# Half of the up projection's low weight parts made by an adding transfer in place of VectorE's subtraction

## The chip, the core and the metric

The kernel runs on one core of one Trainium2 chip. The metric is device time in microseconds (us): three runs of the kernel before took 1555.34, 1555.97 and 1557.21 us, median 1555.97. Beside them stands one profiled execution, from which all rows of the profile come.

## The reference, cut to what matters

The reference is one decoder layer on 256 tokens of 2048 channels in float32: two token mixers (a gated linear recurrence and a sliding-window attention), a gated merge, an output projection, and a squared-ReLU MLP with 8192 hidden channels. The change is in the MLP's first product:

```python
h = rmsnorm(x, norm_mlp_pre[l])
u = jnp.square(jax.nn.relu(h @ w_mlp_up[l]))          # 2048 -> 8192, the up projection
x = x + rmsnorm(u @ w_mlp_down[l], norm_mlp_post[l])  # 8192 -> 2048
```

## The kernel before, in words

Every weight goes through TensorE as two float32r numbers. The high part is the weight rounded to float32r, the low part is what the rounding left (weight minus high part), and a product is put together from matmuls on the high part and on the low part. So each weight is read from memory once and then split on the core.

**The weight stream.** The class `Stream` (line 52) holds all weights as one list of chunks of 128 x 2048 float32 in the order in which TensorE uses them. Each chunk is handled as two halves of 128 x 1024 (512 KB), numbered j = 0, 1, 2 and so on. Three steps stand behind a half:

- `load_to` (L74): SyncE's queue (SP) loads the half into a tile `wraw`. There are WRAW = 4 such buffers for the stream.
- `two_parts` (L92): ScalarE (ACT) copies `wraw` into `whi`, which rounds it to float32r. There are WHALF = 6 buffers of `whi`.
- `two_parts` (L93): VectorE (DVE) subtracts `whi` from `wraw` into `wlo`, of which there are 6 buffers too. With that the `wraw` buffer is free for a later load.

`ahead` runs this up to AHEAD = 6 halves before the half that TensorE (PE) works on; the free buffers decide the rest. A `whi` buffer comes free when PE has done the high matmuls of the half six places earlier, a `wlo` buffer when it has done the low ones.

**The up projection.** It is done in two rounds, f = 0 and f = 1, each of 32 chunks, 64 halves, and each followed by two passes of the down projection over the hidden channels of that round. `a_pair` (line 225) takes four halves: for each half eight matmuls of 512 columns on `whi` (L235), then eight of 256 columns on `wlo` (L238), into the accumulator `ps`. After four halves ScalarE and VectorE take `ps` out (L242, L243), and `evacuate` (L936 to L951) applies ReLU, scale and square and splits the result for the down projection. At the start of f = 0 ScalarE and VectorE also finish the first residual (L914 to L918), which ScalarE's queue stores in eight transfers; the accumulators and that residual are loaded back (L1056, L1057) when the last down passes begin.

**Order.** Each engine works its instructions off in the order in which they stand. A scheduler in the framework sets that order when the program is built, from its own estimates, and it also decides which free buffer a load gets; the kernel pins only a few places. Waits between engines are semaphores. GpSimd (POOL) does four of the low parts at the very start of the program and nothing in the up projection.

Of the kernel before, what the change touches and what calls it, by code (L numbers as in the profile page):

```python
# [16 lines left out]
F32 = mybir.dt.float32  # L17
# [3 lines left out]
ALU = mybir.AluOpType  # L21
# [30 lines left out]
class Stream:  # L52
# [3 lines left out]
    def __init__(self, nc, pool, chunks, room, sums):  # L56
        self.nc, self.pool, self.chunks, self.room, self.sums = nc, pool, chunks, room, sums
        self.raw, self.parts = {}, {}
        self.loaded = self.split = 0
        self.pin = lambda i: i  # L60
        self.low = nc.vector
        self.at = 0

    def load_to(self, n):
        while self.loaded < min(n, 2 * len(self.chunks)):
            j = self.loaded
            c = slice(j % 2 * 1024, j % 2 * 1024 + 1024)
            if j < 2 * EXTRA:
                if j % 2 == 0:
                    self.place = self.room(f"wraw{j}")  # L70
                t = self.place[:, c]
            else:
                t = self.pool.tile([P, 1024], F32, tag="wraw", bufs=WRAW, name=f"wraw{j}")
            self.nc.sync.dma_start(t, self.chunks[j // 2][:, c])  # L74
            self.raw[j] = t
            self.loaded += 1
# [12 lines left out]
    def two_parts(self, src, j):  # L89
        hi = self.pool.tile([P, 1024], F32R, tag="whi", bufs=WHALF, name=f"whi{j}")  # L90
        lo = self.pool.tile([P, 1024], F32R, tag="wlo", bufs=WHALF, name=f"wlo{j}")
        self.pin(self.nc.scalar.copy(hi, src))  # L92
        self.pin(self.low.tensor_tensor(lo, src, hi.bitcast(F32), ALU.subtract))  # L93
        return hi, lo

# [55 lines left out]
def layer(tc, x, pos_t, pos_row, inv_freq, vecs, sinks, gains, w_kv, w_q, w_xy, w_rg, w_g, w_rp, w_ap, w_out,  # L151
# [14 lines left out]
    chunks = [w_kv[i] for i in range(4)]  # L166
# [17 lines left out]
            chunks += [w_g[2 * p + 4], w_g[2 * p + 5]]  # L184
    chunks += [w_out[i] for i in range(16)]
    sums = set()
    for f in range(2):
        chunks += [w_up[32 * f + i] for i in range(32)]
        for n in range(2):
            sums.update(len(chunks) + i for i in SEVEN)  # L190
            chunks += [w_dn[(2 * f + n) * PAIRS + i] for i in range(PAIRS)]

    def unit(name, dt=F32R):
        return big.tile([P, 4, 2, S], dt, tag="U8", name=name)

    def flat(t):
        return t.rearrange("p a b c -> p (a b c)")

    ws = Stream(nc, wpool, chunks, lambda name: flat(unit(name, F32)), sums)

    def units(name):
        return [unit(f"{name}{i}") for i in range(4)]
# [585 lines left out]
    for p in range(8):  # L788
# [8 lines left out]
        hi = mixT[p // 2][:, e : e + 2, 0, :]  # L797
# [222 lines left out]
    for f in range(2):  # L1020
# [3 lines left out]
        for p in range(PAIRS):  # L1024
# [8 lines left out]
            if f == 1 or p >= R2_AT:  # L1033
                for q, u in full:
                    if q in SEVEN:
                        uT[q] = pc.tile([P, 2, 7, P], F32R, tag="seven", bufs=len(SEVEN), name=f"seven{f}{q}")
                    else:
                        i = sum(k not in SEVEN for k in range(q))
# [136 lines left out]
```

## Time and profile before

| | us |
|---|---|
| runs, median of 3 | 1555.97 |
| profiled execution: span from first to last instruction | 1551.8 |
| PE busy | 1520.3 (98%) |
| DVE busy | 1119.6 (72%) |
| ACT busy | 842.6 (54%) |
| POOL busy | 12.1 (1%) |
| L92 `whi`, 528 instructions, mean 1.050 | 548.9 |
| L93 `wlo` on DVE, 524 instructions, mean 1.223 | 635.6 |
| first load of the up weights issued at / last | 815.7 / 1344.5 |

The profiled execution gives its span only; the median of the runs is 4.2 us above it, which is what lies around the span. A row of a group reads: line, engine, operation, output and input tiles, shape, count, busy time and mean ns, then the engine's idle time just before these instructions and what ended it. A row of windows gives the busy time of each engine in a stretch of the span, with the granted clock of TensorE and the busy share of the 16 transfer engines. The two stretches in which PE works on the up projection run from about 847 to 1003 us (f = 0, its first halves split earlier) and from about 1190 to 1370 us (f = 1).

### The profile page before, as it was taken

To read this page: it belongs to the slowest core of one execution; us is meant where nothing else is said; L and a number is where in the kernel's file an instruction comes from. 1 tells how busy PE (TensorE), PEld (TensorE's weight loads), DVE (VectorE), ACT (ScalarE), POOL (GpSimd) and SP (SyncE) were. 2 spreads that over 40 slices of the span, in tenths; PEclk is the share of its full clock that TensorE was granted. 3 is DMA by queue.
4 is the path that set the end of the run, shared out by engine and by line. 5 is a ranking of instruction groups with operands and counts; after the bars stand their busy time and mean duration, and the time that the engine had idled before them with its cause. 6 is when DMAs were issued, how large, how long until landed. Compare 5 with 4: busy or idle time off the path is not lost.

```text
span 1551.8 us, 20965 instructions
## 1 busy us (share of the span) xinstructions
PE 1520.3 (98%) x8042; PEld 1288.1 (83%) x8042; DVE 1119.6 (72%) x1370; ACT 842.6 (54%) x1148; POOL 12.1 (1%) x14
## 2 busy tenths in 40 slices
PE   7999999999999999999999999999999999999996
PEld 5887777788888888888787888888888888888884
DVE  6666667866858877555656876688886766779987
ACT  4545655646647766444354655555454555555552
POOL 3000000000000000000000000000000000000000
PEclk8999999999999999999999999999999999999999
DMA  6554354354655466555663865556667655576564
GB/s 246 170 170 147 125 168 158 126 188 150 227 188 173 162 216 195 190 186 190 252 226 103 274 202 188 189 181 209 212 208 237 205 191 187 182 282 195 202 210 128
DMA packets 82326, 296.26 MB, mean 191 GB/s; under 512 B 9521, under 2 KB 9777, under 8 KB 81201
## 3 DMA queue, kind: packets, MB, share of 16 engines
q1 hardware_dynamic: 78768, 285.48, 56.0%
q10 hardware_dynamic: 3458, 9.45, 1.7%
q8 instruction: 63, 1.03, 0.3%
q14 instruction: 37, 0.30, 0.1%
HBM read 288.60 MB, written 6.29 MB: 190 GB/s over the span
## 4 chain that ended last, share of the span: by engine, by line
PE 83%; DVE 7%; ACT 4%; DMA 4%; issue 2%; POOL 0%; DVEq 0%; ACTq 0%; POOLq 0%
PE ps L235 35%; PE ps L238 18%; PE dQ L956 5%; PE s L956 3%; DVE wlo L93 3%; DMA wraw<-in_w_dn 3%; PE dP L956 3%; PE dCs L956 2%; PE o L253 2%; PE o L255 2%; PE o L257 2%; PE q L253 2%; PE q L255 2%; PE q L257 2%; ACT whi L92 2%
## 5 line engine op out<-in xcount | busy, mean ns | idle before, releaser
L93 DVE TENSOR_TENSOR wlo<-wraw,whi 128x1024 fp32r<-128x1024 f32 x524 | 635.6, 1223 | 312.1 <-ACT whi L92 309.5
L92 ACT CAST whi<-wraw 128x1024 fp32r<-128x1024 f32 x528 | 548.9, 1050 | 571.2 <-PE ps L235 259.7
L235 PE MATMUL ps<-hT,whi 128*128 128x512 f32 x1024 | 261.2, 395 | 0.0
L235 PE MATMUL ps<-h2T,whi 128*128 128x512 f32 x1024 | 256.6, 392 | 0.6 <-DVE h2T L282 0.6
L235 PEld LDWEIGHTS ps<-hT,whi 128*128 128x128 f32 x1024 | 183.8, 189 | 36.0 <-issue 3.1
L235 PEld LDWEIGHTS ps<-h2T,whi 128*128 128x128 f32 x1024 | 184.2, 189 | 33.8 <-DVE h2T L282 0.8
L238 PEld LDWEIGHTS ps<-hT,wlo 128*128 128x128 f32 x1024 | 139.9, 190 | 10.6 <-issue 0.8
L238 PEld LDWEIGHTS ps<-h2T,wlo 128*128 128x128 f32 x1024 | 139.7, 190 | 10.0
L238 PE MATMUL ps<-hT,wlo 128*128 128x256 f32 x1024 | 144.1, 283 | 0.0
L238 PE MATMUL ps<-h2T,wlo 128*128 128x256 f32 x1024 | 142.8, 282 | 0.0
L956 PE MATMUL dQ<-whi,uT 128*128 128x512 f32 x288 | 107.0, 390 | 0.8 <-ACT whi L92 0.8
L235 PE MATMUL ps<-yrnn,whi 128*128 128x512 f32 x256 | 64.4, 393 | 0.7 <-DVE yrnn L748 0.7
L956 PEld LDWEIGHTS dQ<-whi,uT 128*128 128x128 f32 x288 | 54.2, 188 | 12.4 <-ACT whi L92 1.3
L235 PE MATMUL ps<-yatt,whi 128*128 128x512 f32 x256 | 64.1, 392 | 0.0
L956 PE MATMUL dQ<-wlo,uT 128*128 128x512 f32 x144 | 56.5, 392 | 4.0 <-DVE wlo L93 4.0
L112 DVE TENSOR_TENSOR tlo<-t,thi 128x1536 fp32r<-128x1536 f32 x28 | 49.2, 1757 | 9.5 <-ACT thi L111 9.5
L956 PE MATMUL dCs<-whi,uT 128*128 128x512 f32 x144 | 54.6, 396 | 0.0
L956 PE MATMUL dP<-whi,uT 128*128 128x512 f32 x144 | 53.8, 389 | 0.0
L235 PEld LDWEIGHTS ps<-yrnn,whi 128*128 128x128 f32 x256 | 46.0, 189 | 9.3 <-DVE yrnn L748 1.1
L235 PEld LDWEIGHTS ps<-yatt,whi 128*128 128x128 f32 x256 | 46.0, 189 | 8.3
L253 PE MATMUL q<-whi,hT 128*128 128x512 f32 x128 | 51.1, 399 | 0.0
L255 PE MATMUL q<-wlo,hT 128*128 128x512 f32 x128 | 50.4, 393 | 0.0
(255 smaller groups left out, 2068.8 us busy)
## 6 DMA issues: line engine op xcount, KB each, us to landing
wraw<-in_w_up SPq DMA_DIRECT2D x128, 512.0 KB, 4.6
wraw<-in_w_dn SPq DMA_DIRECT2D x128, 512.0 KB, 4.5
wraw<-in_w_g SPq DMA_DIRECT2D x64, 512.0 KB, 4.7
wraw<-in_w_xy SPq DMA_DIRECT2D x64, 512.0 KB, 4.5
wraw<-in_w_q SPq DMA_DIRECT2D x32, 512.0 KB, 4.4
wraw<-in_w_ap SPq DMA_DIRECT2D x32, 512.0 KB, 4.7
wraw<-in_w_rp SPq DMA_DIRECT2D x32, 512.0 KB, 4.8
wraw<-in_w_out SPq DMA_DIRECT2D x32, 512.0 KB, 5.2
```

What stands on the lines that cost most here:

```text
L92: self.pin(self.nc.scalar.copy(hi, src))
L93: self.pin(self.low.tensor_tensor(lo, src, hi.bitcast(F32), ALU.subtract))
L112: v.tensor_tensor(lo, t, hi.bitcast(F32), ALU.subtract)
L235: mm(both, hi[:, k * P : k * P + P], a.rearrange("p a b -> p (a b)"), start=half == 0 and k == 0, stop=False)
L238: mm(ps[:, f, 1, :], lo[:, k * P : k * P + P], a[:, 0, :], start=False, stop=half == 1 and k == 7)
L253: mm(banks[tb][n], a[:, 0, t], hi[:, n * 512 : n * 512 + 512], start=first, stop=False)
L255: mm(banks[tb][n], a[:, 0, t], lo[:, n * 512 : n * 512 + 512], start=False, stop=False)
L257: mm(banks[tb][n], a[:, 1, t], hi[:, n * 512 : n * 512 + 512], start=False, stop=last)
L956: mm(b, a[x], w[y], start=not begun and i == 0, stop=tail and i == 2)
```

## The change

For every odd half of the up projection, 64 of its 128, VectorE's subtraction is taken out. ScalarE writes minus the high part into `wlo` right after it has made `whi`, and a transfer issued by GpSimd adds the raw weights onto it in SBUF (`accum_op=ALU.add`). The sum is the same low part. The even halves, and all other weights, are split as before. In the new file ScalarE's copy stands in L93, its multiplication by -1 in L95, GpSimd's transfer in L96 and VectorE's subtraction in L98.

```diff
     def __init__(self, nc, pool, chunks, room, sums):
...
         self.at = 0
+        self.by_dma = set()
...
         self.pin(self.nc.scalar.copy(hi, src))
+        if j in self.by_dma:
+            self.nc.scalar.mul(lo, hi.bitcast(F32), -1.0)
+            self.nc.gpsimd.dma_start(lo.bitcast(F32), src, accum_op=ALU.add)
+            return hi, lo
         self.pin(self.low.tensor_tensor(lo, src, hi.bitcast(F32), ALU.subtract))
         return hi, lo
...
     sums = set()
+    by_dma = set()
     for f in range(2):
+        by_dma.update(2 * (len(chunks) + i) + 1 for i in range(32))
         chunks += [w_up[32 * f + i] for i in range(32)]
...
     ws = Stream(nc, wpool, chunks, lambda name: flat(unit(name, F32)), sums)
+    ws.by_dma = by_dma
```

The scheduler sets the orders anew. Three places of the up projection show what moved. The numbers behind the tile names are the half (`whi297` is half 297) and then a running number; the names in brackets are the semaphores that an instruction waits for (DMAHW and DMASW: transfers of SP or ACT, and of GpSimd).

ScalarE's queue before, in the middle of f = 0:

```order
L92 CAST whi296_7970<-wraw296_7878 128x1024 [waits DMAHW6_49,PE_49]
L92 CAST whi297_8007<-wraw297_7908 128x1024 [waits DMAHW7_49,PE_49]
L242 COPY u_7902<-ps_7903 128x512 [waits PE_49]
L92 CAST whi298_8029<-wraw298_7930 128x1024 [waits DMAHW0_49,PE_49]
L938 ACTIVATE u_7902<-u_7902 128x512 [waits DVE_49]
L950 CAST seven04_7994<-u_7902 128x384 [waits Activation_49]
L92 CAST whi299_8051<-wraw299_7952 128x1024 [waits DMAHW1_49,PE_49]
L950 CAST seven04_7994<-e_7997 128x512 [waits DVE_49]
L92 CAST whi300_8073<-wraw300_7974 128x1024 [waits DMAHW2_49,PE_49]
```

The same place of ScalarE's queue now:

```order
L93 CAST whi296_7982<-wraw296_7888 128x1024 [waits DMAHW6_49,PE_49]
L93 CAST whi297_8019<-wraw297_7919 128x1024 [waits DMAHW7_49,PE_49]
L250 COPY u_7912<-ps_7913 128x512 [waits PE_49]
L95 ACTIVATE wlo297_8020<-whi297_8019 128x1024 [waits DMASW1_49,Activation_49]
L93 CAST whi298_8042<-wraw298_7941 128x1024 [waits DMAHW0_49,PE_49]
L946 ACTIVATE u_7912<-u_7912 128x512 [waits DVE_49]
L958 CAST seven04_8006<-u_7912 128x384 [waits Activation_49]
L93 CAST whi299_8064<-wraw299_7964 128x1024 [waits DMAHW1_49,PE_49]
L958 CAST seven04_8006<-e_8009 128x512 [waits DVE_49]
L95 ACTIVATE wlo299_8065<-whi299_8064 128x1024 [waits DMASW2_49,PE_49,Activation_49]
L93 CAST whi300_8087<-wraw300_7986 128x1024 [waits DMAHW2_49,PE_49]
```

The multiplication stands between the copy of its own half and that of the next, once behind the copy of `ps` and once behind a cast. GpSimd's queue now holds the adding transfers alone, one for each odd half; before it held nothing here:

```order
L96 DMA wlo293_7915<-wraw293_7821 128x1024 [waits DMASW7_49,DMAHW3_49,PE_49,Activation_49]
L96 DMA wlo295_7960<-wraw295_7866 128x1024 [waits DMAHW5_49,DMASW0_49,Activation_49]
L96 DMA wlo297_8020<-wraw297_7919 128x1024 [waits DMASW1_49,DMAHW7_49,PE_49,Activation_49]
L96 DMA wlo299_8065<-wraw299_7964 128x1024 [waits DMAHW1_49,DMASW2_49,Activation_49]
L96 DMA wlo301_8118<-wraw301_8024 128x1024 [waits DMASW3_49,DMAHW3_49,PE_49,Activation_49]
```

Each transfer waits for the one that filled its `wlo` buffer three odd halves earlier, so `wlo299` waits on DMASW2 for the transfer into `wlo293`, and DMASW2 is the semaphore of half 293, DMASW3 that of half 295. SP's queue, which loads `wraw`, before:

```order
L74 DMA wraw304_8077<-in_w_up 128x1024 [waits DMAHW2_49,DVE_49]
L74 DMA wraw305_8107<-in_w_up 128x1024 [waits DMAHW3_49,DVE_49]
L74 DMA wraw306_8129<-in_w_up 128x1024 [waits DMAHW4_49,DVE_49]
L74 DMA wraw307_8151<-in_w_up 128x1024 [waits DMAHW5_49,DVE_49]
L74 DMA wraw308_8173<-in_w_up 128x1024 [waits DMAHW6_49,DVE_49]
```

SP's queue now:

```order
L75 DMA wraw296_7888<-in_w_up 128x1024 [waits DMAHW1_49,DMASW1_49]
L75 DMA wraw297_7919<-in_w_up 128x1024 [waits DMAHW4_49,DVE_49]
L75 DMA wraw298_7941<-in_w_up 128x1024 [waits DMAHW3_49,DMASW2_49]
L75 DMA wraw299_7964<-in_w_up 128x1024 [waits DMAHW6_49,DVE_49]
L75 DMA wraw300_7986<-in_w_up 128x1024 [waits DMAHW5_49,DMASW3_49]
```

Before, every load waited for VectorE to release the buffer used four halves earlier. Now the load of an even half, 298, takes the buffer of the odd half five places earlier, 293, and waits for that half's adding transfer; the load of an odd half takes the buffer of the even half three places earlier and waits for VectorE.

## The prediction on record

> **What bounds the kernel now.** I read the page first, then the busy times by window over the two stretches of the up projection, then the waits in a quiet part of them, then the timeline of one half, and last the transfers.
>
> ```profile
> span 1551.8 us, 20965 instructions
> PE 1520.3 (98%) x8042; PEld 1288.1 (83%) x8042; DVE 1119.6 (72%) x1370; ACT 842.6 (54%) x1148; POOL 12.1 (1%) x14
> ```
>
> ```profile
> 847.00:1003.00 156.00, 155.39 (x890) 136.67 (x890) 115.23 (x147) 92.82 (x126) 0.00 (x0) 1.00 0.66 211
> 1190.00:1370.00 180.00, 180.00 (x1028) 158.18 (x1028) 125.92 (x149) 99.50 (x121) 0.00 (x0) 1.00 0.60 194
> ```
>
> The columns of a window are its bounds and length, then the busy time of PE, weight load, DVE, ACT and POOL, the granted clock, the share of the 16 transfer engines, and GB/s. TensorE is busy 155.39 of 156 us and 180 of 180 us in the two up stretches, at full clock. Nothing there waits for VectorE or ScalarE but one matmul, at the beginning:
>
> ```profile
> PE ps L235 <- DVE h2T L282: 0.6, 1, 0.6
> ```
>
> Next, in a stretch of 60 us, who waits for whom:
>
> ```profile
> ACT whi L92 <- PE ps L235: 27.5, 22, 1.7
> DVE wlo L93 <- ACT whi L92: 20.1, 22, 1.6
> ```
>
> ScalarE waits for TensorE to release a `whi` buffer, and VectorE waits for ScalarE. The splitting runs as far ahead as its buffers let it, and TensorE sets the pace. The timeline shows one half:
>
> ```profile
> 911.75 1.05 ACT L92 CAST whi<-wraw 128x1024 fp32r<-128x1024 f32 x1 [1.22 <-PE ps L235]
> 912.50 2.00 PE L235 MATMUL ps<-h2T,whi 128*128 128x512 f32 x8
> 912.83 1.22 DVE L93 TENSOR_TENSOR wlo<-wraw,whi 128x1024 fp32r<-128x1024 f32 x1 [0.97 <-ACT whi L92]
> 914.08 3.12 SPq L74 DMA_DIRECT2D wraw<-in_w_up  x2
> 914.34 1.12 PE L238 MATMUL ps<-h2T,wlo 128*128 128x256 f32 x8
> 914.54 1.05 ACT L92 CAST whi<-wraw 128x1024 fp32r<-128x1024 f32 x1 [1.74 <-PE ps L235]
> 915.30 2.00 PE L235 MATMUL ps<-h2T,whi 128*128 128x512 f32 x8
> 915.50 0.59 ACT L242 COPY u<-ps 128x512 f32<-128x512 f32 x1
> ```
>
> A half takes 2.80 us of TensorE (912.50 to 915.30). The subtraction that ends at 914.05 frees a `wraw` buffer and SP issues the next load at 914.08. The high matmuls that end at 914.34 free a `whi` buffer, and the copy begins at 914.54; since there are six buffers, that copy is for the half that TensorE reaches at 912.50 + 6 x 2.80 = 929.30.
>
> **What is removed.** 64 subtractions on VectorE:
>
> ```profile
> L93 DVE TENSOR_TENSOR wlo<-wraw,whi 128x1024 fp32r<-128x1024 f32 x524 | 635.6, 1223 | 312.1 <-ACT whi L92 309.5
> L92 ACT CAST whi<-wraw 128x1024 fp32r<-128x1024 f32 x528 | 548.9, 1050 | 571.2 <-PE ps L235 259.7
> ```
>
> 64 x 1.223 = 78 us of VectorE, which was busy 115 + 126 = 241 of 336 us there and kept nobody waiting. What this can give back is bounded by TensorE's idle time in the stretches: 0.6 us. I take 0.
>
> **What is added on ScalarE.** 64 multiplications of the shape of L92, so 64 x 1.05 = 67 us on an engine busy 92.8 + 99.5 = 192 of 336 us. It would be busy 259, 77%. Each one waits for the low matmuls of the half six earlier, and behind it in the queue stands the next copy. In the timeline the copy ends at 915.59, that `wlo` buffer came free at 915.30, and the copy of `ps` adds 0.59, so the multiplication runs from 916.2 to 917.2. The next copy may begin at 914.54 + 2.80 = 917.34 at the earliest, since it waits for TensorE. The cost is 0, hidden under that wait; without this cover it would be 1.05 us per odd half, 67 us, on an engine that still has 77 us to spare. Placed as it is, I expect none of it on the path.
>
> **What is added on GpSimd and the transfer engines.** 64 transfers of 512 KB that read `wraw`, read `wlo` and write `wlo`. GpSimd stands idle (0.00 in both windows), so nothing is queued behind its waiting instruction but the next such transfer. Two things depend on when the transfer lands: TensorE's low matmuls of that half, and SP's load that takes the `wraw` buffer.
>
> For the matmuls there is room. The multiplication ends at 917.2 and the low matmuls come at 929.30 + 1.84 = 931.1, so the transfer may take 13.9 us.
>
> For the buffer it is tighter. By the order, an even half's buffer goes to the odd half three later, and an odd half's to the even half five later. Two tenancies follow each other in each buffer in 8 halves, or 22.4 us of TensorE. In them stand two loads, two copies, one subtraction, one multiplication and one adding transfer. The loads' durations, from the quiet stretch (920 to 980 us) and from the crowded one (850 to 890 us), in KB and median us to landing:
>
> ```profile
> wraw<-in_w_up SPq DMA_DIRECT2D x22, 512.0 KB, 4.7
> ```
>
> ```profile
> wraw<-in_w_up SPq DMA_DIRECT2D x17, 512.0 KB, 6.3
> ```
>
> ```profile
> 850.00:890.00 40.00, 40.00 (x234) 35.30 (x233) 34.20 (x48) 27.85 (x47) 0.00 (x0) 1.00 0.86 277
> 920.00:980.00 60.00, 60.00 (x347) 52.89 (x346) 39.63 (x50) 32.56 (x40) 0.00 (x0) 1.00 0.57 186
> ```
>
> With the transfer engines 57% busy a load lands in 4.7 us, with 86% in 6.3 us. The adding transfers raise the share from 57%, so I take 5.5, the middle. The sum for 8 halves without the transfer: loads 2 x 5.5 = 11.0, copies 2 x 1.05 = 2.10, subtraction 1.23, multiplication 1.05, half of the 0.59 copy of `ps` = 0.30 (it stands ahead of every second multiplication), and four hand-overs of about 0.1 = 0.4. That is 16.1 us, and leaves 6.3 us for the adding transfer.
>
> No row shows an adding transfer. From below, it is a 512 KB transfer, and the fastest load in the up stretch landed in 3.6 us:
>
> ```profile
> DMA to landing us min/median/max: 3.6/4.7/6.4
> ```
>
> From above, it reads 1024 KB, and the transfers of 1024 KB took:
>
> ```profile
> x<-in_x SPq DMA_DIRECT2D x2, 1024.0 KB, 7.7
> ...
> acc<-acc_away ACTq DMA_DIRECT2D x2, 1024.0 KB, 11.3
> x<-x_away ACTq DMA_DIRECT2D x2, 1024.0 KB, 14.7
> g<-in_gains SPq DMA_DIRECT2D x1, 1024.0 KB, 6.8
> gp<-in_gains SPq DMA_DIRECT2D x1, 1024.0 KB, 10.7
> ```
>
> So it lies between 3.6 and 14.7 us. It cannot be below nothing, since the buffer waits for it in any case. I take 8.5: nearest to the 7.7 and 6.8 of the 1024 KB loads, which also read 1024 KB, and somewhat above, because it runs among other loads all the time, as those of 10.7 and 11.3 did.
>
> That makes 16.1 + 8.5 = 24.6 us for 8 halves against 22.4, 2.2 us too long. Over 128 halves it is 16 x 2.2 = 35 us. Part of it is taken by the lead: the low part may land 13.9 us after the multiplication and needs 8.5, so each stretch can fall behind by 5.4 us before TensorE stands, 10.8 in both. Net: 35 - 10.8 = **24 us**, as waits of TensorE for `whi` and `wlo` late in each stretch. Against the profiled execution: 1551.8 + 24 = 1576 us of span, and with the 4.2 us by which the median of the runs, 1555.97, stands above its span, **1580 us**.
>
> This mechanism's own range: with 5.1 for a load and 7.7 for the transfer the sum is 15.3 + 7.7 = 23.0, 0.6 too long, 10 us in all, which the lead of 2 x 6.2 swallows; with 6.3 and 10.7 it is 17.7 + 10.7 = 28.4, 6.0 too long, 96 - 6 = 90 us. So 1558 to 1646.
>
> **Rival 1: the transfer is hidden.** If it lands within 6.3 us, the two tenancies fit into 22.4 us and TensorE never waits: 1556 us. What speaks for it: TensorE's lead of six halves, the load's own 4.7, and 43% of the transfer engines free. Against it: two reads, and a row at 850 to 890 us where loads alone, with 256 KB stores beside them, already need 86%. There the transfers of the first halves come on top, and the cost may be a few us even then; it is the point at which this case would turn into slower by over 0.2%. The Trainium skill, "DMA: Bandwidth & Descriptors", section "Anatomy of one DMA — SWDGE (gpsimd) path", gives 2.0 us plus bytes over 436 GB/s for a transfer issued by GpSimd, an estimate of 3.2 us here; by that rule the sum is 16.1 + 3.2 = 19.3 and the time 1556. The trace has no such transfer, but its loads, 4.7 us for the same bytes from another queue, are 1.5 us above that estimate, and the rule is for a plain copy. Chance 0.30, of which 0.05 goes to slower by the crowded start.
>
> **Rival 2: the transfer engines become the bound.** What counts then is not how long a transfer takes but how much of the 16 engines.
>
> ```profile
> q1 hardware_dynamic: 3058, 11.12, 57.1%
> ```
>
> ```profile
> 10.00:15.00 5.00, 4.19 (x14) 1.99 (x12) 2.75 (x4) 1.21 (x2) 0.00 (x0) 0.83 1.03 418
> ```
>
> In 60 us 11.12 MB are 21.2 loads of 0.524 MB, and 57.1% of 60 us is 34.3, so a load holds the engines for 1.62 us. With many loads in flight, at the program's start, they moved 418 GB/s, so a load needs at least 1.25 us. Four halves are 11.2 us. Four loads at 1.25 leave 6.2, 3.1 for each of two adding transfers. One that costs a single pass, 1.25, or two, 2.5, fits; three passes of 1.62, 4.9, do not. With 4.0 it would be 5.0 + 8.0 = 13.0, 1.8 too long, 32 x 1.8 = 58, less 10.8 of lead: 47 us, 1603. With 4.9 it is 14.8, 115 - 11 = 104 us, 1660. For it speaks that two reads are needed; against it that source and target lie on the core. The Trainium skill, "Collectives: The Full Stack", section "The bandwidth ceiling: the fold count and why AG ≠ RS ≠ AR", says that an add in a transfer engine costs a second source read and halves the rate; by it an estimate of 2.5 to 3.2 us follows, at the edge of 3.1. No run here shows an add yet. Chance 0.18.
>
> **Rival 3: faster.** VectorE's 78 us free would have to shorten a path on which TensorE waits: the 0.6 us at the start of f = 0, and whatever order the scheduler finds at the edges of the down passes. More than 3 us can hardly come of it. Price -3 us, 1553. Chance 0.05.
>
> **How the numbers follow.** The forecast has 0.47, rival 1 0.30, rival 2 0.18, rival 3 0.05. About 0.2% (3 us) is what a measurement of this kernel can tell from no change. Faster: 0.05. Within it: 0.25. Slower: 0.47 + 0.18 + 0.05 = 0.70. The range reaches from 1553, which takes in the hidden case and rival 3's price, to 1646, the upper end of the forecast's own range; it leaves out the upper part of rival 2 and little else.
>
> **What would show each step.** Right: in the changed profile, L98 in place of L93 with 460 instructions on VectorE, 64 multiplications of 1.05 us, waits of SP's loads of even halves on GpSimd's transfers, ScalarE's copies waiting for `in_w_up` loads where they now wait for PE, and TensorE idle in both up stretches, more towards their ends. In the stretch 920 to 980 the transfer engines should be over 80% busy. Wrong: TensorE at 60 of 60 us there and copies that still wait for PE (rival 1, a landing under 6.3 us); a share of 1.0 with loads landing in 7 us or more (rival 2); ScalarE's multiplications late because TensorE's `wlo` buffers hold them, or GpSimd taking several us to issue one transfer, would be costs that this sum lacks.

## The result: 4.2% slower, and the profile after

The changed kernel takes 1621.0 us (median of 4 runs, 1617.28 to 1629.78) against 1556.6 us: a ratio of 1.0422, interval 1.0403 to 1.0442, or +64 us where +24 was forecast. The time lies in the stated range and on the forecast side of no change, but the loss is 2.7 times the forecast one. The profiled execution has a span of 1618.5 us, 66.7 more than before. Its run took 1620.25 us, so only 1.8 us lie around the span; if it is as much before, the rest of the 4.2 us by which the median there stands above its span is scatter between executions.

Its page, engines first, then the two transfer queues that matter, and the costliest lines:

```profile
span 1618.5 us, 21129 instructions
PE 1543.0 (95%) x8042; PEld 1297.8 (80%) x8042; DVE 1046.5 (65%) x1306; ACT 901.8 (56%) x1212; POOL 67.8 (4%) x78
...
q1 hardware_dynamic: 78768, 285.48, 53.0%
q0 software_dynamic: 9216, 33.56, 11.3%
...
PE 68%; DMA 18%; DVE 5%; issue 5%; ACT 4%; POOL 0%; SPq 0%; DVEq 0%; POOLq 0%; ACTq 0%
...
L98 DVE TENSOR_TENSOR wlo<-wraw,whi 128x1024 fp32r<-128x1024 f32 x460 | 557.9, 1223 | 404.5 <-ACT whi L93 399.7
...
L96 POOL DMA_DIRECT2D wlo<-wraw x64 | 55.6, 869 | 1335.1 <-PE ps L243 854.6
...
L95 ACT ACTIVATE wlo<-whi 128x1024 fp32r<-128x1024 f32 x64 | 67.7, 1058 | 1.0 <-ACT whi L93 0.4
```

The 64 subtractions are gone, the 64 multiplications take 1.06 us each, GpSimd spends 0.87 us on each issue, and transfers now carry 18% of the chain that ends last, against 4%. TensorE is busy 22.7 us longer for the same 8042 matmuls and idle 44.0 us longer. The windows tell where. First the two up stretches of before, then of after, then the first 16 us behind each up stretch of after (columns as in the prediction; a share over 1 can occur because a transfer is counted in the window in which it begins):

```profile
847.70:1027.00 179.30, 179.30 (x1028) 157.81 (x1029) 134.46 (x167) 105.80 (x142) 0.00 (x0) 1.00 0.64 207
1192.10:1370.80 178.70, 178.70 (x1025) 157.27 (x1024) 125.72 (x148) 98.48 (x120) 0.00 (x0) 1.00 0.60 195
```

```profile
849.40:1059.90 210.50, 189.51 (x1028) 161.39 (x1028) 89.83 (x126) 130.31 (x169) 27.89 (x32) 0.97 0.93 247
1232.00:1427.80 195.80, 186.64 (x1035) 160.36 (x1033) 81.59 (x108) 123.62 (x146) 26.90 (x31) 0.98 0.96 254
1059.90:1075.40 15.50, 8.47 (x26) 6.53 (x27) 15.06 (x16) 10.43 (x13) 0.00 (x0) 0.78 0.70 233
1427.80:1444.00 16.20, 8.59 (x24) 6.49 (x24) 14.45 (x15) 10.63 (x13) 0.00 (x0) 0.79 0.66 221
```

The 1028 matmuls of f = 0 take 210.5 us where they took 179.3; TensorE stands 21 us of it and runs the rest more slowly. Behind each up stretch it works only 8.5 of 16 us, at a granted clock of 0.78. The waits of after, by who waits for whom:

```profile
ACT whi L93 <- PE ps L243: 142.6, 97, 3.1
ACT whi L93 <- DMA wraw<-in_w_up: 127.5, 79, 6.2
...
PE ps L246 <- DMA wlo<-wraw: 29.7, 22, 4.1
...
PE s L964 <- DVE u L251: 14.7, 4, 5.2
```

Over the whole execution ScalarE's copies waited 259.7 us for TensorE (the high matmuls) before and 12.0 us for up loads; now it is 142.6 and 127.5. TensorE waits for the adding transfer (29.7 us) and, at the edges, for the evacuation of the last accumulators (14.7). SP's queue and the transfers between 900 and 1000 us show why the loads are late (a load landed in 4.5 us there before):

```profile
SPq L75 <- DMA wlo<-wraw: 54.7, 15, 6.7
SPq L75 <- DVE wlo L98: 15.5, 8, 2.4
```

```profile
q1 hardware_dynamic: 4381, 15.98, 48.5%
q0 software_dynamic: 2226, 8.08, 43.8%
...
wraw<-in_w_up SPq DMA_DIRECT2D x30, 512.0 KB, 6.3
wlo<-wraw POOLq DMA_DIRECT2D x15, 512.0 KB, 7.0
```

SP, which issues the loads, stands 54.7 of 100 us behind adding transfers that have not yet landed. And in 100 us 15.98 MB of loads are 30.5 halves, so a load holds the 16 engines for 48.5 / 30.5 = 1.59 us, and an addition for 43.8 / 15.4 = 2.84.

Cutting each profiled execution at the first and last matmul of the two up stretches gives a table that the experiments below are read by. It holds the differences to the 1551.8 us of before (start 847.7, up f = 0 179.5, edge and down passes 164.9, up f = 1 178.9, edge and tail 180.8). The start moves by 2 us at most, except in e8; e8 and e9 are told below:

| run | ratio to before [interval] | up f = 0 | edge, down | up f = 1 | edge, tail | first down load, us ahead |
|---|---|---|---|---|---|---|
| before | | | | | | 23.7 |
| the change | 1.0422 [1.0403, 1.0442] | +30.9 | +9.3 | +14.8 | +9.9 | 16.2 |
| e1 addition from HBM | 1.0137 [1.0113, 1.0161] | +12.2 | +1.3 | +4.8 | +4.6 | 23.5 |
| e2 multiplication alone | 0.9983 [0.9972, 0.9995] | 0 | +0.1 | 0 | -4.5 | 23.7 |
| e3 copy, no addition | 1.0123 [1.0091, 1.0155] | +8.2 | +8.0 | 0 | +6.8 | 13.4 |
| e4 last 12 by VectorE | 1.0309 [1.0290, 1.0329] | +27.7 | +2.1 | +13.6 | +4.5 | 20.9 |
| e5 copy from HBM | 1.0079 [1.0064, 1.0095] | +3.4 | +3.5 | +1.4 | +2.5 | 23.5 |
| e6 from HBM, last 12 by VectorE | 1.0124 [1.0102, 1.0146] | +14.9 | +0.4 | +4.0 | +1.6 | 23.7 |
| e7 copy, last 12 by VectorE | 1.0082 [1.0060, 1.0103] | +12.7 | +3.9 | +0.7 | -0.1 | 20.9 |
| e10 traffic alone | 1.0191 [1.0167, 1.0215] | +6.8 | +13.4 | +1.6 | +12.8 | 15.8 |
| e11 half the additions | 1.0011 [1.0001, 1.0021] | +3.8 | -0.5 | 0 | +0.2 | 23.8 |
| e12 hold alone | 1.0262 [1.0221, 1.0302] | +10.5 | +12.7 | +2.8 | +11.4 | 8.1 |
| e13 copy and traffic | 1.0439 [1.0400, 1.0477] | +30.7 | +9.1 | +17.5 | +5.8 | 14.2 |
| e14 hold, last 12 by VectorE | 1.0170 [1.0144, 1.0195] | +14.2 | +9.0 | +5.2 | +11.4 | 16.6 |

The last column is the time from SP's issue of the first load for the down passes to the end of the last up matmul of f = 0. For the change those are the rows

```profile
1043.69 29.24 SPq L75 DMA_DIRECT2D wraw<-in_w_dn  x11
...
1058.76 1.11 PE L246 MATMUL ps<-h2T,wlo 128*128 128x256 f32 x8
```

and for before the row `1003.47 36.34 SPq L74 DMA_DIRECT2D wraw<-in_w_dn  x13` with the last up matmul ending at 1027.2. The profiled execution of e14 took 1594 us, 12 more than the median of its runs, so its columns are too high by that much together; that of e7 took 1570.4, 5 more than its median.

### The profile page after: what moved, and what is told of

Read it like the earlier page. It is cut to its first block, busy times and chain, and to the rows that moved or that the text cites. A ratio compares the mean times of both kernels' runs of the same rounds, so it can differ in the third digit from the quotient of the medians.

```text
span 1618.5 us, 21129 instructions
## 1 busy us (share of the span) xinstructions
PE 1543.0 (95%) x8042; PEld 1297.8 (80%) x8042; DVE 1046.5 (65%) x1306; ACT 901.8 (56%) x1212; POOL 67.8 (4%) x78
## 4 chain that ended last, share of the span: by engine, by line
PE 68%; DMA 18%; DVE 5%; issue 5%; ACT 4%; POOL 0%; SPq 0%; DVEq 0%; POOLq 0%; ACTq 0%
PE ps L243 22%; PE ps L246 11%; DMA wraw<-in_w_up 8%; DMA wlo<-wraw 8%; PE dQ L964 8%; PE s L964 4%; PE dP L964 4%; PE dCs L964 3%; PE o L263 2%; PE o L261 2%; PE o L265 2%; PE q L261 2%; DVE wlo L98 2%; ACT whi L93 2%; PE q L263 2%
## 5 line engine op out<-in xcount | busy, mean ns | idle before, releaser
L93 ACT CAST whi<-wraw 128x1024 fp32r<-128x1024 f32 x528 | 548.3, 1048 | 585.7 <-PE ps L243 142.6
L98 DVE TENSOR_TENSOR wlo<-wraw,whi 128x1024 fp32r<-128x1024 f32 x460 | 557.9, 1223 | 404.5 <-ACT whi L93 399.7
L243 PE MATMUL ps<-h2T,whi 128*128 128x512 f32 x1024 | 262.3, 399 | 0.6 <-DVE h2T L290 0.6
L243 PEld LDWEIGHTS ps<-h2T,whi 128*128 128x128 f32 x1024 | 188.3, 193 | 35.1 <-DVE h2T L290 0.8
L246 PE MATMUL ps<-h2T,wlo 128*128 128x256 f32 x1024 | 148.7, 289 | 29.8 <-DMA wlo<-wraw 29.7
L96 POOL DMA_DIRECT2D wlo<-wraw x64 | 55.6, 869 | 1335.1 <-PE ps L243 854.6
L95 ACT ACTIVATE wlo<-whi 128x1024 fp32r<-128x1024 f32 x64 | 67.7, 1058 | 1.0 <-ACT whi L93 0.4
```

The costliest lines, as they stand in the source:

```text
L95: self.nc.scalar.mul(lo, hi.bitcast(F32), -1.0)
L96: self.nc.gpsimd.dma_start(lo.bitcast(F32), src, accum_op=ALU.add)
L243: mm(both, hi[:, k * P : k * P + P], a.rearrange("p a b -> p (a b)"), start=half == 0 and k == 0, stop=False)
L246: mm(ps[:, f, 1, :], lo[:, k * P : k * P + P], a[:, 0, :], start=False, stop=half == 1 and k == 7)
```

## Experiments

Two theories stood at first. **Buffer theory** (the forecast's): the staging buffer `wraw` is held until the addition has landed, so the loads are issued late. **Engine theory** (rival 2): the additions fill the 16 transfer engines. The edges, on which the forecast had no term, are the third question.

**e1: no hold, the same additions.** The adding transfer reads the weights from HBM, so `wraw` is free after ScalarE's copy.

```diff
-            self.nc.gpsimd.dma_start(lo.bitcast(F32), src, accum_op=ALU.add)
+            c = slice(j % 2 * 1024, j % 2 * 1024 + 1024)
+            self.nc.gpsimd.dma_start(lo, self.chunks[j // 2][:, c].bitcast(F32R), accum_op=ALU.add)
```

> The adding transfer reads the weights from HBM once more instead of from wraw, so the wraw buffer of an odd half is free right after ScalarE's copy; the bytes that the transfer engines read and write stay the same. Buffer theory (the forecast's: two loads, the splits and the add in 8 halves of one buffer, 25 us against 22.4): the tenancies shrink to 2 x 6.5 + 2.1 + 1.2 + 0.4 = 17 us and fit, the low part has 13.9 us to land, so 1556 to 1565 us. Engine theory (an add holds the 16 engines for 2.9 us by the profile of the changed kernel, 4 loads x 1.5 + 2 x 2.9 = 11.8 of 11.2 us per four halves, so the engines are full): nothing is relieved, 1605 to 1635 us, share of the engines still 0.93 or more in the up stretches.

1577.3 us, 22 above before: two thirds of the loss are gone, with engines fuller than in the change. The time lies between the two expected ranges, so neither theory has all of it. Windows of 22.4 us of f = 0, three of the change and four of e1:

```profile
916.60:939.00 22.40, 19.72 (x96) 16.91 (x96) 7.42 (x11) 11.79 (x15) 3.47 (x4) 0.85 0.92 229
939.00:961.40 22.40, 20.21 (x115) 17.52 (x116) 9.27 (x12) 14.16 (x17) 2.59 (x3) 1.00 0.94 242
961.40:983.80 22.40, 19.95 (x111) 16.57 (x110) 8.13 (x11) 13.14 (x16) 3.47 (x4) 1.00 0.93 245
```

```profile
847.90:870.30 22.40, 17.71 (x88) 14.82 (x89) 13.77 (x20) 15.81 (x25) 3.63 (x4) 0.92 0.93 248
...
892.70:915.10 22.40, 19.07 (x101) 16.41 (x99) 13.24 (x22) 18.14 (x26) 3.81 (x5) 0.92 0.95 255
915.10:937.50 22.40, 22.40 (x130) 19.72 (x129) 10.31 (x14) 15.97 (x20) 3.64 (x5) 1.00 1.04 290
937.50:959.90 22.40, 22.40 (x130) 19.72 (x129) 11.48 (x15) 15.99 (x20) 3.89 (x5) 1.00 1.04 316
```

With the hold, TensorE stands in every window while the engines are at 0.92 to 0.94: the loads cannot even be asked for. Without it the engines are at 1.04, TensorE runs all 22.40 us, and what it stands falls almost all into the first 70 us, where other transfers still run. Engine theory as the whole explanation falls.

**e2: ScalarE's part alone.** VectorE adds, no transfer.

```diff
-            self.nc.gpsimd.dma_start(lo.bitcast(F32), src, accum_op=ALU.add)
+            self.nc.vector.tensor_tensor(lo, src, lo.bitcast(F32), ALU.add)
```

> ScalarE writes minus the high part as in the change, but VectorE adds the raw weights; no transfer by GpSimd. Buffer and engine theory both put no price on the 64 multiplications: 1556 to 1560 us. A third theory, that the 67 us on ScalarE with its in-order queue delay the copies of whi and of ps: 1570 us or more, with TensorE waiting for ScalarE in the up stretches.

1552.9 us, ratio 0.9983: within the 0.2%, though 3 us under the expected range. The up stretches take as long as before, so the 64 multiplications are hidden, as forecast; why the last stretch is 4.5 us shorter is not shown.

**e3 and e5: the transfer without its addition,** from `wraw` (e3) and from HBM (e5).

```diff
-            self.nc.gpsimd.dma_start(lo.bitcast(F32), src, accum_op=ALU.add)
+            self.nc.gpsimd.dma_start(lo.bitcast(F32), src)
```

```diff
-            self.nc.gpsimd.dma_start(lo, self.chunks[j // 2][:, c].bitcast(F32R), accum_op=ALU.add)
+            self.nc.gpsimd.dma_start(lo, self.chunks[j // 2][:, c].bitcast(F32R))
```

> The same transfer without addition: it copies the raw weights over minus the high part, so the low part is wrong and is left out of the result. Engine theory: a copy reads once and holds the engines about as long as a load, 1.5 us in place of 2.9, so 4 x 1.5 + 2 x 1.5 = 9.0 of 11.2 us: hidden, 1556 to 1568 us, share about 0.8. Buffer theory: the landing falls from 7.0 to about 5 us, and 2 x 5.3 + 5.1 + 5.0 = 20.7 of 22.4 us: hidden too, 1556 to 1568. If it stays above 1600, neither holds, and the price lies in how GpSimd issues a transfer or in the orders.

> The transfer of the run that reads the weights from HBM, without its addition (the low part is then the raw weights, so the addition is left out). With the addition that run was 1577.3 us, 22 above before, although the staging buffer was no longer held. Engine theory of this remainder: an addition held the 16 DMA engines for 2.85 us, a copy for 1.36 us, so that four halves ask 4 x 1.55 + 2 x 1.4 = 9.0 us of 11.2 instead of 11.9; the remainder goes, and the time is 1553 to 1560. Landing theory: the low part comes late because a transfer through GpSimd's queue takes 5 to 8 us from issue to landing whatever it holds; up stretches keep over half of the 17 us that they lost there, and the time is 1565 to 1575.

e3 took 1575.3 us, where both theories had 1556 to 1568; e5 took 1565.9. In both runs the low part is the raw weights. The transfers of e3 between 900 and 1000 us:

```profile
q1 hardware_dynamic: 5177, 18.85, 58.9%
q0 software_dynamic: 2448, 8.91, 23.6%
...
wraw<-in_w_up SPq DMA_DIRECT2D x37, 512.0 KB, 5.5
wlo<-wraw POOLq DMA_DIRECT2D x18, 512.0 KB, 5.8
```

A copy holds the engines for 23.6 / 17.0 = 1.39 us, half an addition's 2.84. With that the up stretch of f = 1 loses nothing and f = 0 loses 8 us, but the edges still cost 15 us. In e5 the up stretches lose 5 us where e1 lost 17, so most of e1's remainder goes with the addition's share of the engines. Between 900 and 1000 us the transfers also land in 5.6 us in place of e1's 8.3, and this run can't part the two; a landing time that stays the same whatever the engines do is ruled out. The time lies in the landing theory's range all the same, because the edges cost 6 us; what that theory said of the up stretches, over half of 17, is wrong.

**e4, e6 and e7: the last 12 halves of each up stretch by VectorE,** in the change, in e1 and in e3.

```diff
-        by_dma.update(2 * (len(chunks) + i) + 1 for i in range(32))
+        by_dma.update(2 * (len(chunks) + i) + 1 for i in range(26))
```

> The change for the first 52 halves of each round only; the last 12 are split by VectorE as before. In the changed kernel the stretch from the end of the up projection to the next stage is 9.2 us longer after f = 0 and 9.7 us longer after f = 1. If these 19 us come from the lag of loads and splits at the end of the up stretch, they go, and with 6 of 32 adds per round less another 46 x 6/32 = 9 us: 1593 us. If they come from the order in which the evacuation of the last accumulator stands among the copies, only the 9 us go: 1612 us.

> The run that reads the weights from HBM for its addition, with the last 12 halves of each up stretch split by VectorE as before. Edge theory (weight buffers held at the end of an up stretch delay the down loads): nothing holds the staging buffer here, so only the lag of the loads under full engines is left at the edges; the 6 us that the two edges cost in that run go, and the up stretches keep their 17 less a tenth to a fifth: 1569 to 1574. If the edges of that run were something else (GpSimd's queue, the order on ScalarE's queue), they stay and the time is 1575 to 1578.

> The copy within SBUF in place of the addition (the addition is left out), with the last 12 halves of each up stretch split by VectorE. The copy alone was 1575.3 us: up +8 and 0, edges +8 and +7. Edge theory: the edges go, the up stretches stay: 1558 to 1563. If the edges come from GpSimd's queue or from lateness built up over the whole stretch, they stay: 1572 to 1577.

e4 took 1602.9 us, e6 1573.5 and e7 1565.3. The edges fall from 19 to 7 us, from 6 to 2 and from 15 to 4, while the up stretches change by some 5 us at most. Only e6 lies in its expected range: e4 lies between its two, because its up stretches gave back 4 us and not 9, and e7 is 2 us above its own (the 4.5 us by which f = 0 got worse stand in a profiled execution that was itself 5 us above the median). So the edge is made in the last halves of the up stretch, not by what stands at the edge. What happens there in the change, on TensorE, ScalarE and VectorE in order of time:

```profile
1059.89 1.04 ACT L93 CAST whi<-wraw 128x1024 fp32r<-128x1024 f32 x1
1061.85 1.05 ACT L93 CAST whi<-wraw 128x1024 fp32r<-128x1024 f32 x1 [0.91 <-DMA wraw<-in_w_dn]
1061.96 0.50 PE L964 MATMUL s<-whi,seven 128*128 128x512 f32 x1 [2.09 <-DVE u L251]
...
1068.15 0.58 ACT L250 COPY u<-ps 128x512 f32<-128x512 f32 x1
...
1069.90 0.69 DVE L251 TENSOR_TENSOR u<-ps,u 128x512 f32<-128x512 f32 x1
...
1070.65 0.79 PE L964 MATMUL s<-thi,seven 128*128 128x512 f32 x1 [4.97 <-DVE u L251]
...
1071.24 0.63 PE L964 MATMUL s<-tlo,seven 128*128 128x512 f32 x1
```

The last accumulator was complete at 1059.87. Its copy stands in ScalarE's queue behind four casts of down weights, the first at 1059.89, and runs at 1068.15, 8.3 us later; TensorE stands for it from 1065.7 to 1070.65. Before, the accumulator was complete at 1027.2:

```profile
1017.90 1.05 ACT L92 CAST whi<-wraw 128x1024 fp32r<-128x1024 f32 x1 [0.60 <-PE ps L235]
...
1028.73 0.58 ACT L242 COPY u<-ps 128x512 f32<-128x512 f32 x1
```

There the same four casts stand ahead of the copy, but the first of them ran 9.3 us before the accumulator was complete, and the copy followed 1.5 us after it. The load of the last of the four landed 4.6 us before the accumulator was complete, in the change 4.5 us after it. So what delays the copy is the loads, not the order of the queue.

**e8 and e10: traffic alone.** VectorE adds, and two more transfers per odd half load the engines; nobody waits for them. In e8 they go from HBM to HBM, in e10 from the high part to HBM.

```diff
+        self.spare = nc.dram_tensor("spare", (2, 8, P, 1024), F32, kind="Internal").ap()
...
-            self.nc.gpsimd.dma_start(lo.bitcast(F32), src, accum_op=ALU.add)
+            self.nc.vector.tensor_tensor(lo, src, lo.bitcast(F32), ALU.add)
+            for s in (0, 1):
+                self.nc.gpsimd.dma_start(self.spare[s, j % 8], hi.bitcast(F32))
```

(in e8 the source is `self.chunks[j // 2][:, c]`)

> The kernel with ScalarE's multiplications and VectorE's additions (1552.9 us, as before), and beside each of the 64 odd halves two transfers of 512 KB from HBM to HBM through GpSimd's queue, whose result nobody uses: the load on the DMA engines without any buffer held and without anyone waiting for the transfer. Engine theory: if the two hold the engines for about the 2.85 us of an addition, the remainder of the HBM run comes back here: 1568 to 1578, with ScalarE waiting for the raw loads in the up stretches. Buffer and landing theories: nothing waits for these transfers, and the loads have 11.2 us for four halves; 1553 to 1560.

> ScalarE's multiplications and VectorE's additions, and beside each odd half two transfers of 512 KB from its high part in SBUF to HBM, through GpSimd's queue; nobody uses them, and they read the high part, so no staging buffer is held for them; unlike those of the traffic run they can't start before the half is copied. Engine theory: the engines get some 2.7 to 3 us per odd half as by an addition, are full, the loads land late: up stretches +10 to +46, 1563 to 1599. Buffer theory: full engines alone stretch the loads to 6 to 7 us, which with short holds (two loads 13, copies 2.1, subtraction and addition 2.5, multiplication 1.1, hand-overs 0.7: 19.4 of 22.4) still fits: up +0 to +6 at the start of a stretch, 1553 to 1562. A delay at the place where the high part's buffer is taken again would show as ScalarE waiting for GpSimd's transfers.

e8 took 1572.5 us (ratio 1.0111 [1.0087, 1.0135]) but says nothing on the question: its transfers depend on nothing in the program, and GpSimd issued them in the first 350 us, where the engines' share rose to 0.95 from 0.50. The up stretches were as before; its profiled execution lost 26 us ahead of them. e10 took 1586.2 us:

```profile
894.80:917.20 22.40, 22.40 (x130) 19.72 (x129) 18.47 (x27) 17.33 (x23) 4.27 (x8) 1.00 1.01 369
917.20:939.60 22.40, 21.47 (x122) 18.54 (x121) 14.63 (x18) 15.84 (x19) 4.26 (x8) 1.00 1.00 372
939.60:962.00 22.40, 21.72 (x124) 18.90 (x124) 14.40 (x18) 15.67 (x19) 4.27 (x8) 1.00 0.99 368
```

Full engines cost TensorE only some 0.5 us in 22.4; the up stretches lose 8 us, the edges 26. That is within engine theory's range in total, but not as it meant it: the loads land in 7.5 us, TensorE hardly stands, and the bill comes at the edge. In f = 0 ScalarE waits 49.3 us for loads and never for these transfers, so no buffer that they read explains it.

**e9, e12 and e14: hold alone.** After VectorE's addition something keeps `wraw`. In e9 it is arithmetic on the buffer, by VectorE once and by GpSimd twice; in e12 two chained transfers of 64 KB inside the buffer; e14 is e12 with `range(26)` as above.

```diff
+            for e in (self.nc.vector, self.nc.gpsimd, self.nc.gpsimd):
+                e.tensor_tensor(src, src, hi.bitcast(F32), ALU.subtract)
```

```diff
+            for c in (128, 256):
+                self.nc.gpsimd.dma_start(src[:, c : c + 128], src[:, c - 128 : c])
```

> No transfer at all: ScalarE's multiplication, VectorE's addition, and then three instructions on the staging buffer itself (one by VectorE, about 1.2 us, two by GpSimd, about 2.4 us each, by the rows of its subtractions in the first stage) whose result nobody uses: after ScalarE's copy the buffer of an odd half is held for 1.06 + 1.23 + 1.23 + 4.8 = 8.3 us and the hand-overs, about as long as by the addition (1.06 + 7.0), with nothing more on the DMA engines. Buffer theory: two loads of 5.0 to 5.5 us, two copies 2.1, the even half's subtraction 1.23, 8.3 and some 0.7 of hand-overs are 22.3 to 23.3 us against 22.4 of TensorE: 0 to 0.9 too long, 0 to 14 us, and ScalarE's copies wait for loads in the up stretches: 1553 to 1568. If the hold alone costs nothing, the long loads under full engines are needed too. Engine theory: nothing, 1551 to 1556.

> The run with the hold alone again, without GpSimd's arithmetic, which slowed VectorE: ScalarE's multiplication and VectorE's addition, and then two transfers of 64 KB through GpSimd's queue inside the staging buffer, the second reading what the first has written, whose result nobody uses. Estimate from GpSimd's issues of 0.87 us and the shortest landings of larger transfers (3.8 us): each 3 to 4 us, the buffer is held 1.06 + 1.23 + 6 to 8 = 8.3 to 10.3 us after the copy, and the DMA engines get 1/4 of a copy's 1.36 us. Buffer theory with loads of 5.2 to 5.5 us: 22.4 to 25.4 us against 22.4: up stretches +0 to +35 with ScalarE waiting for raw loads, 1555 to 1595. Engine theory: 1551 to 1557. If hold and full engines are needed together: near the lower end of the buffer theory, 1555 to 1570.

> The hold by small transfers (1592.1 us; up stretches +10.5 and +2.8, edges +12.7 and +11.4 against before), with the last 12 halves of each up stretch split by VectorE as before. In that run TensorE was busy 98.99 of 100 us in the middle of f = 0, but the first down load was issued only 8.1 us before the last up matmul ended, against 23.7 us before. Lead theory (the hold eats the lead of the loads while TensorE hardly waits, and the lead is missed at the edge): with 12 halves on short holds, 33.6 us of TensorE at 7.4 to 8.3 us of buffer time per half, the lead grows back; first down load 18 to 24 us ahead, edges +0 to +4 each, up stretches as they were: 1565 to 1574. If the edges come from something else, GpSimd's queue or the order on ScalarE's, they stay: 1585 to 1593.

e9 took 1775.3 us (ratio 1.1405) and is spoilt: GpSimd's instructions took 3.25 us in place of the 2.49 of its subtractions at the start of the program and slowed VectorE beside them, so that two engines were the bound. e12 took 1592.1 us; between 900 and 1000 us:

```profile
900.00:1000.00 100.00, 98.99 (x565) 86.62 (x564) 66.05 (x84) 70.20 (x87) 18.29 (x34) 1.00 0.62 203
```

```profile
wraw<-in_w_up SPq DMA_DIRECT2D x34, 512.0 KB, 4.8
wraw<-wraw POOLq DMA_DIRECT2D x34, 64.0 KB, 2.8
```

With the engines at 0.62 the hold costs 13 us in the up stretches and 24 at the edges. This is the clearest view of where the forecast's "lead" went. TensorE stands 1 us in 100, but the loads fall ever further behind it: the first down load is issued 8.1 us ahead of the end, against 23.7. e14 took 1582.5 us, between the two expectations: 12 halves brought the lead back to 16.6 us, not to the 18 to 24 expected. At 16.6 us its edge costs what it costs the change at 16.2 (+9.0 and +9.3); its second edge stays at +11.4. That is the pattern of the whole last column, against the edge behind f = 0: 23 us or more ahead -0.5 to +3.5, 21 ahead +2 to +4, below 17 +8 to +13. Below 17 the cost does not follow the lead any further: e10 pays 13.4 at 15.8 us, e12 12.7 at 8.1.

**e11: half the additions** (`range(0, 32, 2)`).

> Every second one of the additions (32 in place of 64), the rest by VectorE. Buffer theory: over 8 halves the four staging buffers have 4 x 22.4 = 89.6 us; two odd halves with an addition ask 5.5 + 1.05 + 1.06 + 7.0 + 0.7 = 15.3 each, six halves without ask 5.5 + 1.05 + 1.23 + 0.5 = 8.3 each: 80 in all, it fits: up stretches within 4 of before, edges +0 to +6: 1553 to 1563. Engine theory: 4 x 1.55 + 2.85 = 9.0 us of 11.2 per four halves, it fits too. If every addition costs the same whatever the rest does (its lateness, a fixed price), half of the 64 us stays: 1580 to 1590.

1558.6 us, ratio 1.0011. Half the transfers cost a thirtieth of the loss (2 of 64 us): no fixed price per addition, but a limit that is crossed.

**e13: hold and traffic, no addition.** The copy of e3, and one transfer per odd half from the high part to HBM.

```diff
-            self.nc.gpsimd.dma_start(lo.bitcast(F32), src, accum_op=ALU.add)
+            self.nc.gpsimd.dma_start(lo.bitcast(F32), src)
+            self.nc.gpsimd.dma_start(self.spare[j % 8], hi.bitcast(F32))
```

> The copy within SBUF in place of the addition (the addition is left out; alone it was 1575 us, with a landing of 5.7 us and 1.36 us of the engines), and beside it one transfer of 512 KB from the high part to HBM that nobody uses (1.31 us of the engines in the traffic run). Together 2.67 us of the engines, almost the addition's 2.85 to 2.90, and a buffer that is held until a transfer under full engines has landed, but no addition anywhere. Coupled theory (the hold lengthens the cycle, the full engines lengthen loads and hold): nearly the whole loss of the change comes back, 1600 to 1625, with copies landing after 7 us or more and edges of 8 or more each. If the addition itself (its reading and writing) delays beyond its share of the engines: 1575 to 1595.

1618.9 us, ratio 1.0439 [1.0400, 1.0477], against the change's 1.0422 and as the coupled theory had it, but for the second edge (5.8 where 8 or more was expected). The copies land as late as the additions did:

```profile
q1 hardware_dynamic: 4520, 16.48, 51.2%
q0 software_dynamic: 4440, 16.14, 40.1%
...
wlo<-wraw POOLq DMA_DIRECT2D x15, 512.0 KB, 7.1
```

A held buffer and 2.6 us of engines (2 x 40.1 / 30.8) give the whole loss; nothing is left for the addition itself beyond the engine time that it takes. No version here is faster than the kernel before by over 0.2%; e2 and e11 are within it.

## Why the prediction was right in direction and wrong in size

- **What bounds, what is removed, ScalarE's part: right.** e2 gives the three together, 0.9983.
- **The buffer cycle: right as a mechanism.** SP waits for GpSimd's transfers, ScalarE for up loads, and without the hold two thirds of the loss go (e1).
- **The cycle's sum: near by luck.** The transfer landed in 7.0 us where 8.5 was taken, a load in 6.3 where 5.5 was taken. With these and the forecast's other terms, 12.6 + 2.10 + 1.23 + 1.06 + 0.3 + 0.4 + 7.0 = 24.7 us for 8 halves, against its 24.6: two errors that cancel. Measured are 210.4 / 8 = 26.3 in f = 0 and 193.7 / 8 = 24.2 in f = 1, 46 us too long in all where the forecast had 35. The missing part of f = 0 lies in the hand-overs. From the fifth to the 55th half of it the trace gives, on average, 12.4 for two loads, 2.1, 1.2 and 1.1 for copies, subtraction and multiplication, 7.1 for the transfer, and 2.2 for the hand-overs, where the forecast had 0.7: 0.5 ahead of the copies, 0.6 ahead of the multiplication, 0.4 until GpSimd issues, 0.7 until SP issues the next loads. The same sum gives 21.5 for e12, where 23.8 and 22.7 were measured. There the median of 2.8 us hides that the first of the two small transfers landed in 2.4 us on average, the second in 4.4.
- **The step that failed: "Part of it is taken by the lead ... Net: 35 - 10.8 = 24".** The lead of the loads is no reserve that may be used up at the end of a stretch, since the down passes need it, and the prediction put nothing down for the edges. In f = 1 of e12 the up stretch loses only 2.8 us, as the step would have it, but the edge behind it 11.4; in the change the edges cost 19 of 67. Nor was the lead there to use: the sign "more towards their ends" was wrong, since in f = 0 TensorE was short from the first window on:

```profile
849.40:871.80 22.40, 19.05 (x104) 16.05 (x105) 11.75 (x16) 12.54 (x19) 3.62 (x4) 1.00 0.84 224
```

From the forecast 24 to the measured 67 it is 11 for the lead that was taken off, 19 for the edges, 11 for the longer cycle and 2 at the start.

- **A term that was missing, though what it adds is not shown: TensorE's busy time grows with its waits.** Its idle time accounts for only 44 of the 66.7 us; the other 22.7 are longer busy time. Part is a lower clock. In f = 0 of the change the matmuls are busy 189.5 us in place of 179.5, and the granted clock of 0.97 over 210.5 us accounts for 6 to 7 of these 10 us at most. Part is not, since in e3's f = 0 they are busy 181.3 us in place of 179.5 at full clock, with TensorE idle for 6.4:

```profile
847.80:1035.50 187.70, 181.28 (x1028) 157.38 (x1028) 90.56 (x126) 131.17 (x169) 17.17 (x32) 1.00 0.82 278
```

Where the buffer cycle sets the pace, a slower matmul may only fill time in which TensorE would have waited, so the 22.7 us are not a price of their own.

- **Rival 2 was half of it.** It took 4.0 to 4.9 us of the engines for an addition; it was 2.84. That agrees with the rule quoted from the Trainium skill, "Collectives: The Full Stack", section "The bandwidth ceiling: the fold count and why AG ≠ RS ≠ AR", estimate 2.5 to 3.2. The engines were no bound by themselves (0.93 while TensorE stood), but nearly full ones lengthened loads from 4.5 to 6.3 us and the landing of a copy from 5.8 (e3) to 7.1 (e13), and the cycle is made of just these. The prediction had weighed hold and traffic as rivals, 0.47 against 0.18, where they act on one cycle. Their prices are not shown to add up: hold alone +37 and traffic alone +30 come near the change's +64 by luck, since their up stretches lose 13 + 8 us against 46 and their edges 24 + 26 against 19, and e3 (+20) with e10 (+30) is 50 where e13, with half of e10's traffic, lost 64.
- **Rival 1** failed at its landing time: 7.0 us against the 6.3 that would have fitted, and far from the 3.2 estimated from the formula of the Trainium skill, "DMA: Bandwidth & Descriptors", section "Anatomy of one DMA — SWDGE (gpsimd) path", for a plain transfer by GpSimd; even the plain copy of e3 landed in 5.8 beside the loads.

## What to carry to other kernels

A transfer that reads a staging buffer extends that buffer's tenancy by its whole landing time and slows the loads that the buffer waits for; put both into one sum, with landing times at the share of the engines that the change itself will bring about, and with hand-overs as the trace has them. A lead that a stage uses up is not a gain: find who needs it at the stage's end, and see how far ahead the next stage's first load is issued. Do not add up the prices of two causes that were measured one at a time when both act on one cycle.

## What the runs showed of the hardware that was not expected

- **An adding transfer within SBUF holds the 16 engines twice as long as a copy:** 2.84 us against 1.39 for 512 KB, and 1.59 for a load of the same size from HBM.
- **TensorE's clock after a gap.** Behind 4.97 us of idling a 128x512 matmul took 0.63 us in place of 0.39, from 1070.65 to about 1075; behind 2.09 us the first took 0.50 and the next 0.40. The Trainium skill, "TensorE: Matmul & The Clock Gate", section "Part 1: The HAM clock gate (the "warmup" mystery)", has the array fall to half its clock after an idle window of about 3.4 us and need about as long a busy one to return. The first wait agrees, with 4.4 us of slow matmuls behind it, but the trace also has the fall behind a wait that is shorter than such a window, 2.36 us: eight matmuls took 2.04 us in place of 1.11, and full speed was back by 881.75.

```profile
877.30 2.04 PE L246 MATMUL ps<-h2T,wlo 128*128 128x256 f32 x8 [2.36 <-DMA wlo<-wraw]
...
881.75 1.11 PE L246 MATMUL ps<-h2T,wlo 128*128 128x256 f32 x8
```

- **GpSimd and VectorE slow each other.** In e9 VectorE's additions took 2.28 us in place of 1.22, its scaling of `u` 1.93 in place of 0.69, and GpSimd's subtractions 3.25 in place of 2.49; VectorE's addition of the accumulator `ps` kept its 0.68. The Trainium skill, "GPSIMD Engine Reference", section "8. Key points", names contention with VectorE's instructions that have two SBUF inputs; the run agrees and gives it a size.
- **Small transfers are not short.** 64 KB inside SBUF through GpSimd's queue took 2.8 us to land (median between 900 and 1000 us of e12; 1.8 to 7.7 over the run), on engines that were 62% busy; 512 KB took 5.8 in e3, on engines 83% busy.
